# Twelve column pairs of projections move into the seven-product stage, and attention into a stage of its own

## The chip, the cores and the metric

The kernel runs on one core of one Trainium2 chip. The metric is the device time of one execution in microseconds (us). Five engines work in parallel, each through its own queue in order: TensorE (PE, matmuls, with its weight loads PEld), VectorE (DVE), ScalarE (ACT), GpSimd (POOL) and SyncE (SP, which here issues nearly all loads). All transfers share 16 DMA engines. The time before is 2117.61 us, the median of 3 runs (2116.65 to 2117.98).

## The reference, cut to what matters

One layer of a streaming encoder for 512 prompt tokens and 8 streams of 16 new tokens, together 640 columns when tokens lie along the free dimension.

```
h = rms_norm(x, g_pre)                      # 640 x 2048
p = h @ w_in                                # 13312 columns = 104 blocks of 128:
    # 6 stick-breaking heads: q, k, v, gate     24 blocks
    # 6 chunk-band heads:     q, k, v, gate     24 blocks
    # 4 memory heads:         q, gate            8 blocks
    # 3 merge gates of 2048                     48 blocks
o_sb = stick_breaking(q, k, v)   # prompt: causal; samples: 512 cached rows + 16 new
o_bd = band_softmax(q, k, v, rel_bias)      # the same lengths
o_mm = softmax_cross(q, mem_k, mem_v)       # 256 memory rows
merged = sigmoid(mg_sb) * ((o_sb * silu(g_sb)) @ w_up_sb) + ...bd + ...mm
y = x + rms_norm(merged @ w_out, g_post)
```

All is float32. Keys and values of the new tokens are outputs too, for the 12 causal heads.

## The kernel before, in words

Every float32 operand of a matmul is split into a high and a low part (`split`: ACT casts the high part, DVE subtracts), and a product is three matmuls, high by high, high by low, low by high. x lies transposed in four quarter tiles `b11`, `b12`, `b21`, `b22`: the two halves of the 2048 contraction rows by the two halves of the 640 tokens (320 each), 8 blocks of 128 rows in each.

There are two ways to project a block of 128 columns of `w_in`:

- `x_proj` (through `proj`): 16 row blocks, 3 products, 2 token halves: 96 matmuls of 128x320 into an accumulator `acc`, of which there are two. Its weights come in two loads of 512 KB into `wr`, a ring of three buffers, so one buffer feeds 48 matmuls.
- `gate_pair`: two blocks at once by Strassen's way (Winograd's form) with seven products of quarter operands, each 8 row blocks by 3 matmuls of 128x320: 168 matmuls for two blocks, where `x_proj` takes 192. It needs sums of quarter tiles of x (`t1` to `t4`) and, for every pair, sums of quarter tiles of the weights, which POOL forms (`comb`).

The stages are: a prologue (norms, memory keys and values); attention, head by head; the merge gates; the up-projections of the three branches (`up`); the output projection. In the attention stage each causal head runs `x_proj` four times (gate, v, q, k), and each memory head twice; the attention of a head is made of short matmuls that wait for ACT, DVE and POOL between them, and the projections of the next head stand between them on PE. The sums of x are formed in the heads by POOL and kept in DRAM (`t_d`). The merge gates start with four blocks by `x_proj` (`FIRST = 4`), while `t_d` is read back, and go on with 22 pairs.

The order on each engine is set by the framework's list scheduler when the kernel is built, from the dependencies, the tile buffers and some explicit `issue_after` marks; all loads of weights, caches and strips go through SP's one queue, in the order that it set. A head's caches are 16 loads of 128 KB for the keys (`kc`, two buffers of four loads each) and 8 of 256 KB for the values (`vc`).

## Time and profile before

The profiled execution took 2115.59 us, of which 2113.9 us lie between its first and last instruction (the span). The stages, by busy time of each engine in the stretch, granted PE clock (1.00 is full) and mean busy share of the DMA engines:

| stretch, us | stage | PE us (matmuls) | DVE us | ACT us | POOL us | clock | DMA share |
|---|---|---|---|---|---|---|---|
| 82 to 1101 | attention, 60 blocks by `x_proj` | 1017.32 (7779) | 473.87 | 347.36 | 140.16 | 1.00 | 0.60 |
| 1101 to 1140 | into the pairs | 32.54 (193) | 26.28 | 19.26 | 12.33 | 0.91 | 0.70 |
| 1140 to 1650 | pairs | 510.00 (3479) | 278.05 | 232.75 | 234.86 | 1.00 | 0.33 |
| 1650 to 1669 | into the up-projections | 16.02 (104) | 8.87 | 7.65 | 0.00 | 1.00 | 0.60 |
| 1669 to 1886 | up-projections | 215.87 (1463) | 117.21 | 57.72 | 57.70 | 1.00 | 0.55 |
| 1886 to 2114 | output projection | 218.82 (963) | 78.70 | 54.01 | 8.04 | 0.99 | 0.34 |

A matmul's record begins before the one ahead has ended, so its mean duration (310 ns for 128x320) is not what it costs; the number of matmuls in a stretch in which PE never waits is.

### The profile page before, as it was taken

To read this page: it belongs to the slowest core of one execution; us is meant where nothing else is said; L and a number is where in the kernel's file an instruction comes from. 1 tells how busy PE (TensorE), PEld (TensorE's weight loads), DVE (VectorE), ACT (ScalarE), POOL (GpSimd) and SP (SyncE) were. 2 spreads that over 40 slices of the span, in tenths; PEclk is the share of its full clock that TensorE was granted. 3 is DMA by queue.
4 is the path that set the end of the run, shared out by engine and by line. 5 is a ranking of instruction groups with operands and counts; after the bars stand their busy time and mean duration, and the time that the engine had idled before them with its cause. 6 is when DMAs were issued, how large, how long until landed. Compare 5 with 4: busy or idle time off the path is not lost.

```text
span 2113.9 us, 36193 instructions
## 1 busy us (share of the span) xinstructions
PE 2081.3 (98%) x14285; PEld 1975.8 (93%) x14285; DVE 1039.0 (49%) x1686; ACT 775.3 (37%) x1472; POOL 457.5 (22%) x479
## 2 busy tenths in 40 slices
PE   7999999999999999999998999999999999999998
PEld 5999999999999999999998999999999999998886
DVE  5634444544544544454356555555555434582234
ACT  6533333333333333333344444444444322232221
POOL 0001001201202200210024444444444002350000
PEclk9999999999999999999999999999999999999999
DMA  6756555745764763765545333333332655442225
GB/s 227 226 135 148 127 143 137 173 137 131 174 168 107 182 165 92 178 147 145 144 129 170 125 105 105 105 105 122 127 120 66 205 148 159 146 153 80 80 83 216
DMA packets 576153, 297.99 MB, mean 141 GB/s; under 512 B 277330, under 2 KB 537442, under 8 KB 574446
## 3 DMA queue, kind: packets, MB, share of 16 engines
q1 hardware_dynamic: 564158, 261.58, 46.0%
q0 software_dynamic: 4912, 18.37, 2.3%
q10 hardware_dynamic: 6912, 15.73, 1.9%
q8 instruction: 112, 1.84, 0.4%
q14 instruction: 59, 0.48, 0.1%
HBM read 254.18 MB, written 41.43 MB: 140 GB/s over the span
## 4 chain that ended last, share of the span: by engine, by line
PE 94%; DMA 3%; DVE 1%; ACT 1%; issue 0%; SPq 0%; DVEq 0%; ACTq 0%
PE acc L169 49%; PE q L750 25%; PE ya L156 3%; PE ya L157 3%; PE ya L155 3%; PE s L526 2%; PE o L577 1%; DMA r<-t_d 1%; PE tp L449 1%; PE acc L157 1%; DMA or<-osg_d 1%; PE acc L156 1%; PE o L156 1%; PE acc L155 1%; PE s L155 0%; PE o L155 0%
## 5 line engine op out<-in xcount | busy, mean ns | idle before, releaser
L100 DVE TENSOR_TENSOR wl<-wr,wh 128x512 fp32r<-128x512 f32 (+1 forms) x548 | 421.8, 774 | 558.0 <-ACT wh L99 554.2
L99 ACT CAST wh<-wr 128x512 fp32r<-128x512 f32 (+1 forms) x548 | 330.9, 608 | 745.9 <-PE acc L169 456.5
L169 PE MATMUL acc<-xl,wh 128*128 128x320 f32 x1920 | 452.1, 311 | 0.0
L169 PE MATMUL acc<-xh,wl 128*128 128x320 f32 x1920 | 448.5, 311 | 0.0
L169 PE MATMUL acc<-xh,wh 128*128 128x320 f32 x1920 | 441.1, 310 | 1.7 <-DVE qm L359 1.7
L169 PEld LDWEIGHTS acc<-xl,wh 128*128 128x128 f32 x1920 | 323.6, 188 | 15.3 <-issue 14.7
L169 PEld LDWEIGHTS acc<-xh,wh 128*128 128x128 f32 x1920 | 321.9, 188 | 3.9 <-DVE qm L359 2.2
L169 PEld LDWEIGHTS acc<-xh,wl 128*128 128x128 f32 x1920 | 323.1, 188 | 1.9 <-issue 1.6
L100 DVE TENSOR_TENSOR wl<-ws,wh 128x512 fp32r<-128x512 f32 x176 | 153.4, 874 | 139.7 <-ACT wh L99 139.4
L750 PE MATMUL q<-xl,wh 128*128 128x320 f32 x704 | 218.4, 310 | 1.4 <-DVE xl L100 1.4
L750 PE MATMUL q<-xh,wh 128*128 128x320 f32 x704 | 218.5, 310 | 0.3 <-ACT xh L99 0.3
L750 PE MATMUL q<-xh,wl 128*128 128x320 f32 x704 | 218.3, 310 | 0.2 <-DVE wl L100 0.2
L99 ACT CAST wh<-ws 128x512 fp32r<-128x512 f32 x176 | 109.3, 622 | 170.7 <-PE q L750 152.2
L750 PE MATMUL q<-th,wh 128*128 128x320 f32 x528 | 163.7, 310 | 4.0 <-ACT th L99 4.0
L750 PE MATMUL q<-tl,wh 128*128 128x320 f32 x528 | 163.7, 310 | 0.7 <-DVE tl L100 0.7
L750 PE MATMUL q<-th,wl 128*128 128x320 f32 x528 | 163.5, 310 | 0.0
L750 PEld LDWEIGHTS q<-xl,wh 128*128 128x128 f32 x704 | 133.2, 189 | 1.6 <-DVE xl L100 1.6
L750 PEld LDWEIGHTS q<-xh,wh 128*128 128x128 f32 x704 | 133.0, 189 | 0.6 <-ACT xh L99 0.5
L750 PEld LDWEIGHTS q<-xh,wl 128*128 128x128 f32 x704 | 133.1, 189 | 0.4 <-DVE wl L100 0.4
L155 PE MATMUL ya<-wh,gh 128*128 128x512 f32 x320 | 124.7, 390 | 0.0
L157 PE MATMUL ya<-wh,gl 128*128 128x512 f32 x320 | 124.7, 390 | 0.0
L156 PE MATMUL ya<-wl,gh 128*128 128x512 f32 x320 | 124.7, 390 | 0.0
(223 smaller groups left out, 3013.0 us busy)
## 6 DMA issues: line engine op xcount, KB each, us to landing
wr<-in_w_in_dram SPq DMA_DIRECT2D x208, 512.0 KB, 4.6
wr<-in_w_out_dram SPq DMA_DIRECT2D x32, 512.0 KB, 3.8
sig_d<-sig ACTq DMA_DIRECT2D x48, 320.0 KB, 4.4
sig<-sig_d SPq DMA_DIRECT2D x48, 320.0 KB, 3.4
kc<-in_cache_sb_k_dram SPq DMA_DIRECT2D x96, 128.0 KB, 3.3
vc<-in_cache_sb_v_dram SPq DMA_DIRECT2D x48, 256.0 KB, 4.8
kc<-in_cache_band_k_dram SPq DMA_DIRECT2D x96, 128.0 KB, 3.4
vc<-in_cache_band_v_dram SPq DMA_DIRECT2D x48, 256.0 KB, 5.5
```

The source lines that it names most:

```text
L99: ACT.copy(hi, src)
L100: DVE.tensor_tensor(lo, src, hi.bitcast(F32), op=ALU.subtract)
L155: PE.matmul(out, ah, bh, start=start, stop=False)
L156: PE.matmul(out, ah, bl, start=False, stop=False)
L157: PE.matmul(out, al, bh, start=False, stop=stop)
L169: PE.matmul(acc[:, s, :HF], a[:, k], b[s], start=first and f, stop=last and l)
L449: PE.transpose(tp[:, kb * P:(kb + 1) * P], b[:, kb * P:(kb + 1) * P], ident)
L526: return PE.matmul(s[32 * j:32 * j + 32, :nc_], qm[:, j, par * 32:par * 32 + 32], kts[j], start=par == 0, stop=par == 1, tile_position=(0, ...
L577: PE.matmul(o[32 * j:32 * j + 32, :P], l, r, start=i == 0, stop=i == len(steps) - 1, tile_position=(0, 32 * j))
L750: PE.matmul(bank_, a[:, k], b[:, k], start=first and k == 0 and n == 0, stop=k == KH - 1 and n == 2, skip_group_check=not first)
```

## The change

The chunk-band heads' 24 blocks leave `x_proj`. `gate_pair` becomes `block_pair(col, put)`, and 12 pairs for q, k, v and gate of the six chunk-band heads are run by it ahead of the 22 gate pairs; `put_raw` writes each block to DRAM (`raw_d`, 24 tensors of 320 KB), the gate block as x times its sigmoid. The whole stage of pairs moves to the front, between the prologue and attention; four gate blocks by `x_proj` stand at its start, and `sums` forms the sums of x beside them on DVE and POOL straight into the split operands, without DRAM. `t3` still takes the place of `b12`; the plain sum of b12 is kept in DRAM (`b12_d`), and the last pair takes its products in another order, reads b12 back and splits it again. The first projection of attention then starts with the second half of the rows (`back`).

In attention, a chunk-band head loads its four blocks (`loaded`) from `raw_d` in place of projecting them. `sample_att` is cut in two, `sample_score` and `sample_out`, and a head's prompt attention and scores are woven with the `sample_out` of the head before it. Heads run in the order 0, 6, 1, 7, 12, 2, 8, 3, 9, 13, 4, 5, 14, 15, 10, 11 (0 to 5 stick-breaking, 6 to 11 chunk-band, 12 to 15 memory). Buffers `b` and `e` go from 1 to 2, `l0` and the new-token tiles to 2; one of the four PSUM banks gets a tag of its own. The up-projections take the branches in the order stick-breaking, memory, chunk-band, and the first of them are free to start once the last `x_proj` matmul has been issued.

```
-B = dict(wr=3, wh=4, wl=4, kc=2, kt=4, vc=8, b=1, e=1, raw=1, q=1, k=1, v=1, wt=1)
+B = dict(wr=3, wh=4, wl=4, kc=2, kt=4, vc=8, b=2, e=2, raw=1, q=1, k=1, v=1, wt=1)
...
-    t_d = dpool.tile([4, P, KH, HF], F32, name="t_d")
+    b12_d = dpool.tile([P, KH, HF], F32, name="b12_d")
+
+    raw_d = [[dpool.tile([P, NT], F32, name=f"raw_d{n}_{h}") for h in range(6)] for n in range(4)]
...
+    def bank(name, own=False):
+
+        return ps_a.tile([P, 512], F32, tag="ps" if own else "pa", name=name, bufs=1 if own else 3)
...
+    def loaded(n, h):
+        t = pa.tile([P, NT], F32, tag=f"l{n}", name=f"l{n}", bufs=2 if n == 0 else 1)
+        SP.dma_start(t, raw_d[n][h])
+        return t
+
+    def transposed(col, n, raw):
+
+        if raw is not None:
+            return loaded(n, raw)
         acc = new_acc()
         x_proj(col, acc)
...
-    def sums(k):
-
-        r = pa.tile([P, 4, HF], F32, tag="sums", name="sums")
-        r1, r2, r3, r4 = (r[:, n] for n in range(4))
-        with tc.issue_after(last_on(POOL)):
-            for t, q in ((r1, b11), (r3, b12), (r2, b22), (r4, b21)):
-                POOL.tensor_tensor(t, q[0][:, k].bitcast(F32), q[1][:, k].bitcast(F32), op=ALU.add)
-        for t, x, y in ((r1, r3, r1), (r3, r2, r3), (r2, r2, r1), (r4, r4, r2)):
-            POOL.tensor_tensor(t, x, y, op=ALU.subtract)
-        POOL.dma_start(t_d[:, :, k].rearrange("n p c -> p n c"), r)
...
+    def sums(k):
+
+        r2, r1, r4 = (sw.tile([P, 2, HF], F32, tag="ws", name="rs", bufs=3) for _ in range(3))
+        r3 = staged(k < 6)
+        ks = slice(k, k + 2)
+        for eng, t, q in ((DVE, r1, b11), (POOL, r2, b22), (DVE, r3, b12), (POOL, r4, b21)):
+            eng.tensor_tensor(t, q[0][:, ks].bitcast(F32), q[1][:, ks].bitcast(F32), op=ALU.add)
+        POOL.dma_start(b12_d[:, ks], r3)
+        for eng, t, x, y in ((POOL, r1, r3, r1), (POOL, r3, r2, r3), (POOL, r2, r2, r1), (DVE, r4, r4, r2)):
+            eng.tensor_tensor(t, x, y, op=ALU.subtract)
+        for t, r in ((t1, r1), (t2, r2), (t4, r4)):
+            split(t[0][:, ks], t[1][:, ks], r)
+        return lambda: split(t3[0][:, ks], t3[1][:, ks], r3)
+
+    third = []
     for i in range(FIRST):
         gate(i)
+        third.append(sums(2 * i))
...
+    def put_raw(n, h):
+        def put(b, t, q):
+            if q is not None:
+                ACT.copy(t[:, :HF], q)
+            if n == 3:
+                u = sw.tile([P, NT], F32, tag="sl", name="sl")
+                ACT.activation(u, t, AF.Sigmoid)
+                POOL.tensor_tensor(u, u, t, op=ALU.mult)
+                t = u
+            POOL.dma_start(raw_d[n][h + b], t)
+        return put
+
+    pairs = [(C_BD + 768 * n + h * P, put_raw(n, h)) for n in range(4) for h in range(0, 6, 2)]
+    pairs += [(C_GATE + i * P, put_gate(i)) for i in range(FIRST, 3 * KB, 2)]
+    for n, (col, put) in enumerate(pairs):
+        block_pair(col, put, n == 0, n == len(pairs) - 1)
...
+        for h in (0, 6, 1, 7, 12, 2, 8, 3, 9, 13, 4, 5, 14, 15, 10, 11):
+            prompt, score, out = causal_head(h) if h < 12 else mem_head(h - 12)
+            interleave(rest, prompt, score)
+            rest = out
...
-        with tc.issue_after(mark if 1 < i < KB else first):
+        with tc.issue_after(mark if i > 1 else last_mm):
             proj(w_up[0], j * P, nh, o_src, acc)
```

Three places show how the order moves. The first is SP's queue around the loads of a chunk-band head (`wr` weights, `kc` cached keys, `vc` cached values, `l` a block read from `raw_d`, `natk` the prompt's keys written out). Before:

```order
L126 DMA wr<-in_w_in_dram 128x8x128 x2
L511 DMA kc<-in_cache_band_k_dram 32x32x32 x8
L126 DMA wr<-in_w_in_dram 128x8x128
L511 DMA kc<-in_cache_band_k_dram 32x32x32 x8
L126 DMA wr<-in_w_in_dram 128x8x128 x2
L504 DMA vc<-in_cache_band_v_dram 128x4x128 x8
```

And of the change, for head 9:

```order
L128 DMA wr<-in_w_in_dram 128x8x128 x2
L495 DMA kc<-in_cache_band_k_dram 32x32x32 x8
L128 DMA wr<-in_w_in_dram 128x8x128
L495 DMA kc<-in_cache_band_k_dram 32x32x32
L353 DMA l_13555<-raw_d_2_114 128x640
L495 DMA kc<-in_cache_band_k_dram 32x32x32 x6
L629 DMA out_dram<-natk 32x16x32 x4
L353 DMA l_13572<-raw_d_2_108 128x640
L495 DMA kc<-in_cache_band_k_dram 32x32x32
L546 DMA vc<-in_cache_sb_v_dram 128x4x128 x8
L128 DMA wr<-in_w_in_dram 128x8x128 x2
```

Between the two first weight loads and the last two stood one weight load, 16 key loads; now all 16 key loads, the reads of `raw_d`, the writes of `natk` and the 8 value loads of the head before stand there, with one weight load among them.

The second is PE in the prompt attention of a stick-breaking head, from the transposes `tp` of one query block over the scores `s` of the next. Before (32 projection matmuls of `acc` follow before the next `tp`, of which the first five stand here):

```order
L449 MATMUL tp<-ident,b 128x128 x2
L155 MATMUL s<-kh,qh 128x256
L156 MATMUL s<-kl,qh 128x256
L157 MATMUL s<-kh,ql 128x256
L169 MATMUL acc<-xh_79,wl 128x320
L169 MATMUL acc<-xh_75,wh 128x320
L169 MATMUL acc<-xh_79,wh 128x320
L169 MATMUL acc<-xl_76,wh 128x320
L169 MATMUL acc<-xl_80,wh 128x320
```

And of the change, in head 2, the one place of this kind in a causal head:

```order
L438 MATMUL tp<-ident,b 128x128 x2
L158 MATMUL s<-kh,qh 128x256
L159 MATMUL s<-kl,qh 128x256
L160 MATMUL s<-kh,ql 128x256
L510 MATMUL s<-kt,qm_10309 32x512 x4
L438 MATMUL tp<-ident,b 128x128
L158 MATMUL o<-wth,vh 128x256
L522 MATMUL s_13513<-knT,qr 128x128
L614 MATMUL t_13558<-ident,l_13555 128x128 x4
L510 MATMUL s<-kt,qm_10309 32x512 x4
L173 MATMUL acc<-xh_73,wh 128x320
```

No projection matmul stands between `s` and the `tp` that follows from it there, nor between that `tp` and the `o` that follows from it.

The third is POOL. Before, the sums of x stand in the heads:

```order
L659 TENSOR_TENSOR sums<-xh_73,xl_74 128x320
L659 TENSOR_TENSOR sums<-xh_77,xl_78 128x320
L659 TENSOR_TENSOR sums<-xh_79,xl_80 128x320
L659 TENSOR_TENSOR sums<-xh_75,xl_76 128x320
L661 TENSOR_TENSOR sums<-sums 128x320 x4
L662 DMA t_d<-sums 128x4x320
```

Now the last of the four sums (`rs`, `rx`) stands right ahead of the weight sums of the first pair (`ws`):

```order
L698 TENSOR_TENSOR rs<-rx,rs 128x640
L695 TENSOR_TENSOR rs<-xh_79,xl_80 128x640
L695 TENSOR_TENSOR rs<-xh_77,xl_78 128x640
L698 TENSOR_TENSOR rx<-rs,rx 128x640
L698 TENSOR_TENSOR rs<-rs 128x640
L730 TENSOR_TENSOR ws<-wr 128x512
L730 TENSOR_TENSOR ws<-wr,wr_1485 128x512
L730 TENSOR_TENSOR ws<-ws,wr 128x512 x2
```

All 20 of POOL's operations on the sums of x come ahead of the first weight sum, in the time of the four gate blocks.

More of the change, by code (lines that the diff above doesn't have):

```diff
@@ L157, in mm3, with proj @@
         PE.matmul(out, al, bh, start=False, stop=stop)
-    def proj(w, col, kn, src, acc, half=8):
-        for k0 in range(0, kn, half):
+    def proj(w, col, kn, src, acc, half=8, back=False):
+        starts = range(0, kn, half)
+        for i0, k0 in enumerate(reversed(starts) if back else starts):
             n = min(half, kn - k0)
@@ L626, in causal_head @@
-        spill(sg, i)
+        raw = h if kind == "bd" else None
+        sg = head_g(c0 + 2304 + h * P, raw)
+        vt = transposed(c0 + 1536 + h * P, 2, raw)
+        nat = pa.tile([P, 4, P], F32, tag="nat", name="nat")
+        t0 = bank("t0")
+        for t in range(4):
+            PE.transpose(t0[:, t * P:(t + 1) * P], vt[:, t * P:(t + 1) * P], ident)
+        DVE.tensor_copy(nat, t0.rearrange("p (t n) -> p t n", t=4))
+        POOL.dma_start(vp.rearrange("(t p) e -> p t e", p=P), nat)
+        vn = natural_new(vt, vs, "vn")
@@ new lines, in causal_head @@
+        qt = transposed(c0 + h * P, 0, raw)
+        kt = transposed(c0 + 768 + h * P, 1, raw)
+        v = split_v(nat)
+        qh, ql, qr = split_q(qt)
+        kh = pa.tile([P, TP], F32R, tag="kh", name="kh")
+        kl = pa.tile([P, TP], F32R, tag="kl", name="kl")
+        split(kh, kl, kt[:, :TP])
+        nat = pa.tile([P, TP], F32, tag="nat", name="natk")
+        DVE.transpose(nat, kt[:, :TP])
+        for a in range(4):
+            SP.dma_start(kp[:, 32 * a:32 * a + 32].rearrange("(c i) j -> i c j", i=32),
+                         nat[32 * a:32 * a + 32].rearrange("p (c j) -> p c j", j=32))
@@ L769, in gate_pair @@
         add(o0[:, lo], qb)
-        if i == FIRST:
+        if first:
             for f in third:
                 f()
-            fourth = [load_sum(4, t4, k, SP) for k in (0, 2)]
         product(qa, s2, t2, False)
         ACT.copy(o0[:, hi], qa)
-        if i == FIRST:
-            for f in fourth:
-                f()
-            fourth = [load_sum(4, t4, k, SP) for k in (4, 6)]
+        if last:
+            product(qa, s3, t3, False)
+            ACT.copy(o1[:, hi], qa)
+            for k in range(0, KH, 2):
+                r = staged(k % 4 == 0)
+                SP.dma_start(r, b12_d[:, k:k + 2])
+                split(b12[0][:, k:k + 2], b12[1][:, k:k + 2], r)
         qc = half()
         product(qc, s1, t1, True)
-        ACT.copy(o1[:, hi], qc)
+        if last:
+            add(o1[:, hi], qc)
+        else:
+            ACT.copy(o1[:, hi], qc)
         s4 = s2
```

252 lines of the change are left out of this document (103 added, 149 removed).

## The prediction

> **What bounds the kernel now.** I read the engines' busy time first, then the chain of work that ended last, then the stages by windows.
>
> ```profile
> PE 2081.3 (98%) x14285; PEld 1975.8 (93%) x14285; DVE 1039.0 (49%) x1686; ACT 775.3 (37%) x1472; POOL 457.5 (22%) x479
> PE 94%; DMA 3%; DVE 1%; ACT 1%; issue 0%; SPq 0%; DVEq 0%; ACTq 0%
> 82.00:1101.00 1019.00, 1017.32 (x7779) 972.02 (x7778) 473.87 (x882) 347.36 (x696) 140.16 (x260) 1.00 0.60 147
> 1200.00:1250.00 50.00, 50.00 (x343) 50.00 (x342) 26.88 (x35) 22.67 (x41) 23.89 (x17) 1.00 0.34 111
> 1100.00:1150.00 50.00, 43.54 (x268) 41.60 (x267) 35.91 (x43) 24.78 (x43) 18.91 (x13) 0.93 0.58 184
> 1650.00:1700.00 50.00, 46.91 (x313) 45.71 (x312) 20.24 (x33) 14.69 (x27) 0.00 (x0) 1.00 0.69 215
> 450.00:500.00 50.00, 49.34 (x355) 46.69 (x357) 23.90 (x43) 17.45 (x36) 3.67 (x12) 1.00 0.41 96
> 800.00:850.00 50.00, 48.97 (x398) 46.25 (x398) 23.89 (x43) 14.66 (x33) 2.55 (x9) 1.00 0.40 97
> 1750.00:1800.00 50.00, 49.36 (x333) 48.57 (x332) 20.42 (x32) 11.39 (x22) 16.65 (x10) 1.00 0.51 144
> ```
>
> PE sets the pace: 94% of the chain is PE, and in 1019 us of attention it is idle 1.7 us, nearly all of it from 450 to 500 and from 800 to 850. Where nothing else is in the stream (1200 to 1250), 343 matmuls of 128x320 pass in 50 us, so one costs **0.1458 us**. The 60 projected blocks of the attention stage are 60 x 96 x 0.1458 = 840 us of its 1019, and its attention matmuls the other 179. PE loses time at two seams: 343 - 268 = 75 matmuls or 10.9 us going into the pairs (1100 to 1150), and 343 - 313 = 30, or 4.4 us, going into the up-projections (1650 to 1700), with 1.5 us more where their second branch starts (1750 to 1800).
>
> **The change, part by part.** *Matmuls removed.* Twelve pairs take 168 where x_proj takes 192: 12 x 24 = 288 fewer, x 0.1458 = **-42.0 us**. This is on the path wherever PE stays the pace-setter. Nothing is removed from the attention matmuls.
>
> Rows for the work of POOL, for a wait that goes away, and for a DVE split that was held up beside POOL's weight sums:
>
> ```profile
> L842 POOL TENSOR_TENSOR merged<-merged,sig 128x640 f32<-128x640 f32 x32 | 59.7, 1869 | 193.4 <-DVE sig L841 177.5 <-DMA sig<-sig_d 14.4 <-issue 1.5
> L743 POOL TENSOR_TENSOR ws<-ws,wr 128x512 f32<-128x512 f32 x44 | 66.0, 1521 | 15.9 <-DVE wl L100 15.9
> 1115.64 0.63 PE L750 MATMUL q<-th,wh 128*128 128x320 f32 x1 [3.60 <-ACT th L99]
> 1094.84 5.25 DVE L100 TENSOR_TENSOR wl<-wr,wh 128x512 fp32r<-128x512 f32 x1 [1.24 <-ACT wh L99]
> ```
>
> *The longer stage of pairs.* 34 pairs x 168 x 0.1458 = 833 us. DVE, ACT and POOL are busy 27, 23 and 24 of 50 us there. A chunk-band pair does the same splits and weight sums as a gate pair; it swaps a sigmoid for a copy, and for the gate block POOL adds one product of 640 (1.9 us by the first row). POOL also issues the writes to raw_d, 2 in 24.5 us. The first two weight sums of the next pair stand ahead of these writes in POOL's queue, so I cost this at nothing; PE's 24.5 us per pair hide it. Without that cover it would be about 2 us for each of the three gate pairs.
>
> *The first seam.* Reading t_d back goes away, and with it waits like the third row; the sums of x now run beside the four gate blocks. POOL does 20 operations of 640 x 1.87 = 37 us and then four weight sums x 1.52 = 6 us before the third product of the first pair can be split. Cover: 4 x 96 x 0.1458 = 56 us of gate blocks and two products of 24, 7 us, so 63 against 43 plus the waits for the splits between the sums (each set of three buffers is used again, some 2 us x 3) and for b12_d to be written. It fits with perhaps 10 us to spare, unless DVE is held up as in the last row, where one split took 5.25 us beside POOL's work. Ends: all 10.9 us gained, or none. I take **-5 us**. At the far end of the stage b12 is read back and split under three products (10.5 us) and the 48 matmuls of the second half of the rows (7 us): nothing.
>
> *The second seam.* The order puts up-projection matmuls among the last heads, so osg is read earlier. Ends: the 4.4 and 1.5 us gained, or none: **-5 us**.
>
> *Attention with less to hide behind.* Of the 60 blocks 24 go to the pairs and the four gate blocks ahead of them, so its PE work falls to 32 x 96 x 0.1458 + 179 = 448 + 179 = 627 us. What must fit beside it:
>
> ```profile
> 1669.00:1886.00 217.00, 215.87 (x1463) 214.62 (x1464) 117.21 (x148) 57.72 (x104) 57.70 (x31) 1.00 0.55 164
> 350.00:400.00 50.00, 50.00 (x369) 48.52 (x369) 27.20 (x52) 18.36 (x39) 12.62 (x19) 1.00 0.76 182
> L100 DVE TENSOR_TENSOR wl<-wr,wh 128x512 fp32r<-128x512 f32 x516 | 408.2, 795 | 558.0 <-ACT wh L99 554.2 <-DMA out_dram<-natk 1.3
> t_d<-sums POOLq DMA_DIRECT2D x8, 640.0 KB, 5.9
> kc<-in_cache_band_k_dram SPq DMA_DIRECT2D x96, 128.0 KB, 3.4
> vc<-in_cache_band_v_dram SPq DMA_DIRECT2D x48, 256.0 KB, 5.5
> SPq L126 <- DVE wl L100: 324.2, 70, 9.6
> SPq L511 <- DVE kt L522: 82.2, 24, 8.0
> SPq L504 <- PE o L577: 34.3, 24, 6.3
> 867.89 6.24 SPq L511 DMA_DIRECT2D kc<-in_cache_band_k_dram  x8
> 875.30 7.68 SPq L511 DMA_DIRECT2D kc<-in_cache_band_k_dram  x8
> 889.33 5.98 SPq L504 DMA_DIRECT2D vc<-in_cache_band_v_dram  x8
> 898.15 0.37 SPq L126 DMA_DIRECT2D wr<-in_w_in_dram  x1
> 901.88 1.98 SPq L383 DMA_DIRECT2D out_dram<-natk  x4
> ```
>
> DVE: 474 less 112 splits (28 blocks x 4) x 0.795 = 385 us, 61% of 627. DMA: 0.60 x 1019 = 611 us of all 16 engines. The up-projections move their bytes at 0.55 / 164 = 3.35 us per MB; by that price the 28 blocks' weights (29.4 MB) take 98 us away, t_d's 5.2 MB 17 us, and reading raw_d (24 x 0.33 MB) adds 26. That leaves 522 us in 627, a share of **0.83**. The highest 50 us of attention before stood at 0.76, with PE never waiting, so 0.76 is no ceiling, but 0.83 as a mean is not shown. The work left on each queue fits; what can go wrong is its order.
>
> The order gives two bounds. From below: one causal head has no projection between its scores and its transposes, and the change from memory head 15 has a few such steps.
>
> ```profile
> 646.09 0.28 PE L157 MATMUL s<-kh,ql 128*128 128x256 f32 x1
> 648.65 0.42 DVE L464 TENSOR_TENSOR b<-b,e 128x255 f32<-128x255 f32 x1
> ```
>
> From the last score matmul to the end of the weights of a 256-wide block takes 3.0 us here; in head 2 some 11 short matmuls, 1.3 us, stand in between, and after it a 128-wide block and a split come uncovered: about 4 us there and 3 us at head 15, 7 in all. Everywhere else 4 us or more of matmuls stand in such a gap. From above: SP's stretch for a chunk-band head. I take 7 us and as much again for transfers that come late in the densest part (heads 12, 2, 8, 3, of which the three causal ones bring 4 MB of caches each): **+15 us**; ends 0 and +60 (first rival).
>
> **The sum**, against the profiled execution: -42 - 5 - 5 + 15 = -37 us on 2115.6 (span 2113.9 and 1.7 around it) is 2078.6; the median of the runs shown is 2 us above the profiled one, so **2080 us**.
>
> **The rivals.** *First, slower: weights wait behind the caches in SP's queue.* Among 16 key loads (0.87 us each by the rows), 2 reads of raw_d and one weight load (0.37), 4 writes (0.5) and 8 value loads (0.75), SP issues for 14 + 1 + 2 + 6 = 23 us with one weight load among them. Three buffers of 48 matmuls and that one give PE 28 us. If the key loads meet their longest wait (8.0 us) and the value loads theirs (6.3), it is 37 us, and with some 2 us until the data is split PE stands 11 us; six chunk-band heads make 66 us: 2117.6 - 52 + 15 + 66 = **2147 us**. It decides from 37 / 6 = 6 us per chunk-band head. For it: SP is in order, and the key buffers hold half a head (8 of 16 loads), so the later ones wait for DVE's transposes. Against: attention's own 11 us per head also feed PE, and before, SP waited 324 us for weight buffers, so it was mostly ahead.
>
> *Second, nothing stalls:* the gaps are filled, both seams close: 2117.6 - 42 - 10.9 - 5.9 = **2059 us**. For it: PE idle 1.7 us in 1019 before.
>
> *Third, the seams stay and attention loses more:* the sums of x arrive late behind POOL and DVE, up-projections still wait, and stalls are 25 us: 2117.6 - 42 + 25 = **2101 us**. For it: the 5.25 us row. Against: 20 us between 43 and 63.
>
> *Fourth, stalls that slow the clock.* After an idle time the trace shows lower clock:
>
> ```profile
> 1110.00:1125.00 15.00, 10.08 (x51) 8.59 (x50) 7.95 (x12) 6.51 (x11) 9.24 (x7) 0.89 0.59 190
> ```
>
> With the 3.60 us wait of the row above, these 15 us passed 51 matmuls of 103 at a clock of 0.89. If the 15 us of new stalls come in one or two pieces of that length, each followed by 0.11 x 15 = 1.7 us lost to the clock, and matmuls beside them stay sparse, the loss is nearer to 25 us: **2090 us**. [...]
>
> **How the numbers follow.** Chances: forecast 0.52, slower rival 0.13, nothing stalls 0.15, seams 0.12, clock 0.08. The forecast's own range, from 0 to 50 us of stalls, is 2066 to 2116; the range to the other cases takes in the second, third and fourth rivals and leaves out most of the first: 2052 to 2116. A measurement of this kernel tells 0.2%, 4 us. Faster needs less than 2113.4: all but the first rival and the forecast's and third's worst ends, 0.82; within 4 us 0.04; slower 0.14.
>
> **What would show it.** Right: 343 matmuls in each 50 us of a stage of pairs some 833 us long; attention with clock 1.00, a DMA share near 0.8 and PE waits of 10 to 20 us, the largest at heads 2 and 15; no wait of some us at the first `t2` product. The first rival shows as PE waiting for ACT or DVE splits of `wr` in attention, ahead of it SP waiting for `kc` or `vc` buffers; the third as waits for `tl`, `th` or `ws` at the start of the pairs, and for `oh` at the up-projections. The forecast is wrong if attention takes over 665 us, or if the pairs pass fewer than 343 matmuls per 50 us.

## The result, and the profile after

The changed kernel takes **2135.3 us** (median; 2131.4 to 2138.2) against 2117.3 us of the kernel before on the same chip: a ratio of 1.0084, 95% interval [1.0066, 1.0101]. It is 0.8% slower; 2080 us was forecast, and the range ended at 2116. The profiled execution took 2134.1 us, its span is 2132.4.

The page of the changed kernel, engines and chain of waits:

```profile
PE 2058.5 (97%) x13997; PEld 1945.9 (91%) x13997; DVE 1128.3 (53%) x1788; ACT 815.5 (38%) x1567; POOL 599.0 (28%) x557
PE 85%; issue 4%; DMA 4%; DVE 2%; POOL 2%; SPq 2%; ACT 1%; DVEq 0%; POOLq 0%; ACTq 0%
```

The 288 matmuls are gone (14285 - 13997), but PE's share of the chain fell from 94% to 85%: PE waits now. Where it does is read from the windows of the changed kernel (stretch; PE, PEld, DVE, ACT, POOL busy; granted clock, DMA share, GB/s), by stage first:

```profile
78.00:134.40 56.40, 56.40 (x386) 56.36 (x386) 47.03 (x38) 22.44 (x35) 40.42 (x26) 1.00 0.45 144
134.40:980.80 846.40, 842.23 (x5714) 841.25 (x5714) 477.96 (x590) 375.40 (x670) 424.24 (x307) 0.99 0.35 112
980.80:1614.10 633.30, 604.33 (x4686) 560.00 (x4685) 315.84 (x624) 219.58 (x472) 56.95 (x150) 0.98 0.71 165
1614.10:1764.00 149.90, 126.50 (x988) 115.69 (x987) 85.50 (x179) 49.33 (x111) 9.32 (x26) 0.92 0.76 199
1764.00:1905.10 141.10, 140.66 (x959) 140.40 (x958) 70.60 (x102) 39.47 (x70) 55.71 (x32) 1.00 0.58 167
...
500.00:550.00 50.00, 50.00 (x343) 50.00 (x343) 26.48 (x34) 23.07 (x41) 23.87 (x17) 1.00 0.34 111
100.00:150.00 50.00, 45.83 (x286) 45.06 (x285) 46.40 (x34) 19.53 (x33) 40.37 (x22) 0.90 0.35 111
1100.00:1150.00 50.00, 41.43 (x275) 38.96 (x274) 21.52 (x47) 14.19 (x31) 3.18 (x8) 0.90 0.91 204
1650.00:1700.00 50.00, 37.24 (x264) 34.72 (x265) 26.47 (x53) 11.48 (x29) 2.64 (x7) 0.85 0.90 224
```

The rows are: four gate blocks, pairs, attention up to the last projected block, its last heads with up-projections among them, the rest of the up-projections. Inside the pairs 343 matmuls pass per 50 us, as forecast. From 100 to 150, where the pairs begin, 57 are missing (8.3 us). Attention and up-projections take 924 us (980.8 to 1905.1). Worked out for them were 627 us and the 217 us of the row from 1669 to 1886 before, but that row holds 1463 of the 1536 matmuls of the up-projections; with the other 73, at 0.1458 us each, it is 627 + 228 = 855, so **some 69 us are lost**. PE stands idle for 53 of them (29.0 + 23.4 + 0.4, from the busy times). That leaves about 16 for the lower clock, 0.98 over 633 us and 0.92 over 150. So the whole gain of the pairs, and some, goes into attention.

What PE waits for from 1100 to 1150 must be read through two queues. PE's waits name a softmax, but the chain of waits of the changed kernel goes on behind it (start, duration, piece):

```profile
1112.19 0.11 PE o L158
1112.29 5.73 DMA vc<-in_cache_band_v_dram
...
1118.09 5.28 DMA wr<-in_w_in_dram
...
1126.46 0.36 DVE b L463
```

and the timelines of DVE and of ACT there show both idle for 14.3 us ahead of the same weight split (in brackets the idle time and what ended it):

```profile
1124.11 0.69 DVE L102 TENSOR_TENSOR wl<-wr,wh 128x512 fp32r<-128x512 f32 x1 [14.35 <-ACT wh L101]
1124.72 0.42 DVE L432 SCALAR_TENSOR_TENSOR b<-s,strip 128x256 f32<-128x256 f32 x1
```

```profile
1123.46 0.62 ACT L101 CAST wh<-wr 128x512 fp32r<-128x512 f32 x1 [14.29 <-DMA wr<-in_w_in_dram]
```

The scores were ready (PE had passed them by 1112.7); their softmax stood behind the split of a weight slab in DVE's in-order queue, and that slab's load had only been issued at 1118.09. SP's timeline of the changed kernel says why:

```profile
1059.73 17.15 SPq L128 DMA_DIRECT2D wr<-in_w_in_dram  x3
1080.90 6.93 SPq L495 DMA_DIRECT2D kc<-in_cache_sb_k_dram  x8
1087.92 3.17 SPq L598 DMA_DIRECT2D st<-rext_d  x6
1091.19 8.53 SPq L495 DMA_DIRECT2D kc<-in_cache_sb_k_dram  x4
1099.82 1.10 SPq L594 DMA_DIRECT2D st<-rext_d  x1
1101.03 0.97 SPq L495 DMA_DIRECT2D kc<-in_cache_sb_k_dram  x2
1102.09 2.40 SPq L629 DMA_DIRECT2D out_dram<-natk  x4
1104.53 1.38 SPq L495 DMA_DIRECT2D kc<-in_cache_sb_k_dram  x2
1105.95 1.56 SPq L594 DMA_DIRECT2D st<-rext_d  x3
1107.61 5.48 SPq L546 DMA_DIRECT2D vc<-in_cache_band_v_dram  x8
1113.15 2.76 SPq L594 DMA_DIRECT2D st<-rext_d  x4
...
1118.09 1.01 SPq L128 DMA_DIRECT2D wr<-in_w_in_dram  x2
```

SP has issued the weight loads of the first row by 1076.9, and the next one follows at 1118.1. In these 41 us stand 4 us of waiting for a key buffer, key loads (17.8 us of issuing, 5.75 of them in one load), value loads (5.5), writes (2.4) and 16 small strip loads (9.5). The three weight buffers feed 3 x 48 matmuls, 21 us, and attention's own work 11 us at most; then everything behind the weights stands.

Not all of the idle time is of this kind. Three such stretches in attention are longer than 28 us: 41 us (here), 36 us from 1300 and 57 us from 1591. Inside them and in the 10 us after each, PE stands idle for 9.5, 0.9 and 19.6 us, 30 of the 52 us that it is idle from 981 to 1764. The middle one costs next to nothing. Elsewhere the chain of waits runs through late cache loads themselves, as here, where PE then stood idle for 4.3 us:

```profile
1208.39 6.99 DMA kc<-in_cache_sb_k_dram
```

A key load takes 3.4 us in the median of the run; this one, and another of 6.77 us at 1420.65, landed late, their transposes on DVE came late (DVE idles 2.96 us ahead of those at 1215.39), and what stood behind those in DVE's queue came late for PE.

### The profile page after: what moved, and what is told of

The parts are those of the page before. It is cut to its first block, busy times and chain, and to the rows that moved or that the text cites. A ratio compares the mean times of both kernels' runs of the same rounds, so it can differ in the third digit from the quotient of the medians.

```text
span 2132.4 us, 36113 instructions
## 1 busy us (share of the span) xinstructions
PE 2058.5 (97%) x13997; PEld 1945.9 (91%) x13997; DVE 1128.3 (53%) x1788; ACT 815.5 (38%) x1567; POOL 599.0 (28%) x557
## 3 DMA queue, kind: packets, MB, share of 16 engines
q1 hardware_dynamic: 541310, 265.51, 46.4%
## 4 chain that ended last, share of the span: by engine, by line
PE 85%; issue 4%; DMA 4%; DVE 2%; POOL 2%; SPq 2%; ACT 1%; DVEq 0%; POOLq 0%; ACTq 0%
PE q L737 39%; PE acc L173 26%; PE ya L160 3%; PE ya L158 3%; PE ya L159 3%; PE s L510 1%; POOL merged L864 1%; PE o L569 1%; SPq L495 1%; DMA kc<-in_cache_sb_k_dram 1%; PE tp L438 1%; PE acc L158 1%; PE acc L160 1%; DVE wl L102 1%; PE acc L159 1%
## 5 line engine op out<-in xcount | busy, mean ns | idle before, releaser
L737 PE MATMUL q<-xh,wl 128*128 128x320 f32 x1088 | 338.1, 311 | 4.2 <-DVE wl L102 4.2
L737 PE MATMUL q<-xl,wh 128*128 128x320 f32 x1088 | 337.6, 310 | 0.0
L173 PE MATMUL acc<-xh,wl 128*128 128x320 f32 x1152 | 271.5, 313 | 0.0
L173 PE MATMUL acc<-xh,wh 128*128 128x320 f32 x1152 | 269.2, 313 | 0.0
L173 PE MATMUL acc<-xl,wh 128*128 128x320 f32 x1152 | 269.1, 312 | 0.0
L173 PEld LDWEIGHTS acc<-xh,wh 128*128 128x128 f32 x1152 | 194.4, 189 | 10.4 <-issue 7.5
L173 PEld LDWEIGHTS acc<-xl,wh 128*128 128x128 f32 x1152 | 194.9, 190 | 6.3 <-issue 6.3
L173 PEld LDWEIGHTS acc<-xh,wl 128*128 128x128 f32 x1152 | 195.2, 190 | 2.8 <-issue 2.3
L730 POOL TENSOR_TENSOR ws<-wr 128x512 f32<-128x512 f32 x102 | 148.6, 1470 | 80.0 <-DVE wl L102 78.0
L737 PEld LDWEIGHTS q<-th,wl 128*128 128x128 f32 x816 | 153.2, 188 | 0.2 <-DVE wl L102 0.2
```

Of the source, the lines that this page charges most:

```text
L173: PE.matmul(acc[:, s, :HF], a[:, k], b[s], start=first and f, stop=last and l)
L730: eng.tensor_tensor(o, a[c], b[c], op=op)
L737: PE.matmul(bank_, a[:, k], b[:, k], start=first and k == 0 and n == 0, stop=k == KH - 1 and n == 2, skip_group_check=not first)
```

## The experiments

Two theories of the loss, which the texts on record put at 80 us: **S**, supply (weights, strips and caches come too late for so little PE work), and **C**, chains (the two interleaved heads' own dependencies). All edits are to the changed kernel, and all ratios to the kernel before, timed beside each. The order on every queue is set anew by the list scheduler for each kernel, so an edit that changes costs or buffers also moves instructions.

**1. Half of the move.** Values and gates stay in the pairs; queries and keys go back to `x_proj`:

```
-        qt = transposed(c0 + h * P, 0, raw)
-        kt = transposed(c0 + 768 + h * P, 1, raw)
+        qt = transposed(c0 + h * P, 0, None)
+        kt = transposed(c0 + 768 + h * P, 1, None)
-    pairs = [... for n in range(4) for h in range(0, 6, 2)]
+    pairs = [... for n in (2, 3) for h in range(0, 6, 2)]
```

> Undoes half of the move: only the value and gate projections of the chunk-band heads stay in the stage of pairs, their query and key projections go back to x_proj in attention (the same result). It gives back 6 x 24 x 0.1458 = 21 us of matmuls and returns 12 x 14 = 168 us of projections to attention. Theory S (attention is starved: the transfers, in the order in which SP issues them, do not come in time for so little PE work): DMA 522 + 42 of weights - 13 of raw reads = 551 us in 795, a share of 0.69 instead of 0.83, so most of the 80 us lost between the start of attention and the output projection go: 2135 + 21 - 65 = 2091 us, 2080 to 2105. Theory C (the chains within two interleaved heads starve PE, whatever the transfers do): the loss stays with the heads, 2135 + 21 = 2156 us; above 2140 speaks for C.

Measured: 2096.0 us, 0.9903 [0.9888, 0.9917]; S said 2091, C 2156. Half of the move is faster than the kernel before and than all of it. A window of this kernel from within attention, in which PE is idle for 4 of 600 us:

```profile
900.00:1500.00 600.00, 595.64 (x4643) 559.17 (x4642) 294.71 (x566) 223.74 (x449) 52.49 (x143) 1.00 0.66 155
```

This does not yet decide between the theories: two blocks more in a head give its loads more time, and they also fill the gaps of its chains.

**2. One cache load per head.**

```
-        for b_ in range(NB):
-            t = pa.tile([P, 4, P], F32, tag="vc", ...)
-            SP.dma_start(t, cv[b_]...)
-            vcs.append(t)
+        t = pa.tile([P, 4, P], F32, tag="vc", ...)
+        SP.dma_start(t, cv[0]...)
+        vcs = [t] * NB
 # and kc = load_k(0) once ahead of the loop, instead of four times in it
```

> Leaves out most cache transfers: each head loads one of its four key pieces and one of its eight value caches and uses it for all (other values are computed, the instructions of PE, DVE and ACT stay the same). Theory S: with about 52 MB less to move, attention loses less than 15 us instead of 80: 2060 to 2075 us. Theory C: the loss stays, above 2115 us.

Measured: 2078.9 us, 0.9821 [0.9805, 0.9837]. Without the cache transfers 56 us come back, with as many instructions as before on PE, DVE and ACT (13997, 1788 and 1567): S carries most of the loss. It is 4 us above S's range, though. Bytes, issues and waits for cache buffers go together here, so the run does not tell which of them it is.

**3. The sums of x on DVE alone.**

```
-        for eng, t, q in ((DVE, r1, b11), (POOL, r2, b22), (DVE, r3, b12), (POOL, r4, b21)):
+        for eng, t, q in ((DVE, r1, b11), (DVE, r2, b22), (DVE, r3, b12), (DVE, r4, b21)):
 # and the four subtractions on DVE as well
```

> Moves all sums of x beside the four gate blocks from POOL to DVE (the same result). Theory P (the first seam is late because DVE runs its splits at 1.4 to 2.1 us instead of 0.8 beside POOL's sums): DVE's 32 sums cost 26 us in a window of 56 that then holds 16 x 0.8 of weight splits and 16 x 0.82 of sum splits, 52 in all, and the 58 matmuls or 8.5 us lost between 125 and 150 mostly come back: 2127 to 2131 us. Rival (there is simply too much for DVE before the third product): the same or slower, 2134 to 2142 us.

Measured: 2125.3 us, 1.0050 [1.0033, 1.0067], 10 us less. DVE's groups from 100 to 150 us (busy, mean ns of one), of the changed kernel:

```profile
L102 DVE TENSOR_TENSOR wl<-wr,wh 128x512 fp32r<-128x512 f32 x11 | 20.2, 1849 | 1.5 <-ACT wh L101 1.4
```

and of this kernel, with its window:

```profile
L102 DVE TENSOR_TENSOR wl<-wr,wh 128x512 fp32r<-128x512 f32 x11 | 8.6, 786 | 0.4 <-ACT wh L101 0.4
```

```profile
100.00:150.00 50.00, 50.00 (x343) 50.00 (x342) 47.59 (x54) 22.68 (x37) 18.42 (x12) 1.00 0.40 122
```

Beside POOL's sums (POOL busy 40.4 of 50 us) one weight split takes 1849 ns; without them, with POOL still busy 18.4 us, 786. DVE does 20 operations more in the stretch in nearly the same busy time, 47.6 us where it was 46.4, and the seam closes. What it is in POOL's sums that holds the splits up, these runs do not show.

**4. Keys issued from POOL's queue** (`POOL.dma_start` for `SP.dma_start` in `load_k`).

> Issues the key cache loads from POOL's queue instead of SP's (the same result and bytes). Theory Q (weights stand behind key loads in SP's in-order queue, which wait for buffers or are slow to issue, 1.7 us each in places): weights are issued in time and at least half of the 80 us goes: 2090 to 2105 us. Theory B (the 16 DMA engines themselves are full in these stretches, at shares of 0.8 to 1.04): the order of issue changes little, 2125 to 2145 us; if POOL is slow to issue, more.

Measured: 2133.1 us, 1.0070 [1.0050, 1.0089]: no gain clear of the noise, as B had it, but not for B's reason alone. POOL's busy time rises from 599 to 790 us, and PE's waits for softmaxes from 16 to 21 us. Inconclusive for SP's queue.

**5. Half of the move and the sums on DVE.** The edits of 1 and 3.

> Both at once: value and gate projections of the chunk-band heads in the pairs, query and key projections in attention, and all sums of x on DVE (the same result). If the two losses are separate (the seam at 125 to 150 us, and starved attention), the gains add: 2096 - 7 to 10 = 2087 us, 2083 to 2091. If an earlier start of the pairs is given back later, 2094 us or more.

Measured: 2089.1 us, 0.9874 [0.9859, 0.9888]: 7 us below the half alone. The two losses are separate, as the first forecast had it.

**6. Keys in longer runs.** Each of the four loads of a key tile reads 512-byte rows of a half of one stream instead of 128-byte pieces of two.

> Reads as many bytes of key caches in as many loads, but in runs of 512 bytes instead of 128 (so the keys arrive in another order and the scores of the sample rows are others). By packet times of 13.0 and 28.7 ns, the 16 engines' time for keys falls from 213 to about 118 us. Theory B (the DMA engines are too full in bursts): 95 of the about 262 us of engine time that the run with one cache per head took away, which gave 56 us, so 20 us: 2115 us, 2108 to 2122. Theory W (the key loads wait for buffers that DVE's transposes free, the transfer's own time does not matter): 2129 to 2138.

Measured: 2145.2 us, 1.0135 [1.0117, 1.0154]; neither theory. SP's transfers of the changed kernel and of this one (packets, MB, share of 16 engines):

```profile
q1 hardware_dynamic: 541310, 265.51, 46.4%
```

```profile
q1 hardware_dynamic: 369278, 265.51, 43.3%
```

The engines are relieved by 0.464 x 2132 - 0.433 x 2142 = 62 us, and the time rises by 10. So their time over the whole run is not what attention lacks, and theory B falls as it was stated. But SP's issuing of the keys became shorter as well (for the 96 loads of the stick-breaking heads 58.7 us in all instead of 98.5, by SP's timelines), while a key load lands later (in the median 4.5 us instead of 3.6 for these heads, 4.1 instead of 3.7 for the chunk-band heads), and the order moved. So SP's issuing time alone does not set the loss either, and why this kernel is slower stays open.

**7. A third key buffer** (`kc=3`, and one buffer for the query tile).

> Three key buffers instead of two; for room, one query buffer instead of two (the same result). Theory W (SP stands at key loads until DVE's transposes free a buffer, and weights behind it come late): 2112 to 2125 us. Theory B (full DMA engines): the same, 2130 to 2138.

Measured: 2179.6 us, 1.0298 [1.0282, 1.0313], 44 us *slower* than the change, and neither theory. SP's order where the keys of the first chunk-band head begin, in the changed kernel:

```profile
1027.12 13.28 SPq L128 DMA_DIRECT2D wr<-in_w_in_dram  x3
1040.66 2.98 SPq L495 DMA_DIRECT2D kc<-in_cache_band_k_dram  x3
```

and in this one:

```profile
1025.14 5.80 SPq L495 DMA_DIRECT2D kc<-in_cache_band_k_dram  x4
1031.06 0.49 SPq L128 DMA_DIRECT2D wr<-in_w_in_dram  x1
```

Keys are issued earlier, ahead of weights. Near the end SP issues no weight load for 129 us:

```profile
1592.77 0.62 SPq L128 DMA_DIRECT2D wr<-in_w_up_sb_dram  x1
1593.96 4.66 SPq L546 DMA_DIRECT2D vc<-in_cache_mem_v_dram  x8
...
1722.34 0.43 SPq L128 DMA_DIRECT2D wr<-in_w_up_sb_dram  x1
```

In that stretch SP also waits for results of the last heads (the longest waits are 13.7, 12.5 and 11.8 us), so a part of it belongs to the heads' chains. And the query tile lost a buffer in the same run; which of the two changes of buffers costs the 44 us was not tried.

**8. Another order of heads**: `(0, 6, 1, 7, 2, 8, 3, 9, 4, 10, 5, 11, 12, 13, 14, 15)`.

> Another order of heads only: stick-breaking and chunk-band heads in turn, the four memory heads last (the same result); so the chunk-band heads 10 and 11 no longer stand together at the end, where PE loses some 35 of the 80 us between 1600 and 1700. Theory S: without projections two heads with 8 MB of caches cannot be fed, spread they can: 2108 to 2122 us. Theory C, or a loss that only moves to another pair of heads: 2128 to 2140.

Measured: 2166.2 us, 1.0241 [1.0215, 1.0266], slower than both theories. With heads of both kinds in turn, SP goes six times for 38 to 45 us without a weight load, once for each chunk-band head. The chunk-band heads starve one by one; a neighbour with four projections does not save them.

Runs 6, 7 and 8 pointed at one quantity, read from SP's timeline of each kernel: the stretches between two weight loads (`wr`) in attention, all its rows from the first head to the last, and what they exceed 28 us by, summed. The 28 us are the first rival's three buffers and one, 21 + 7, a threshold that no run measures. The table has all kernels, in the order of that sum; runs 9 to 18 follow below, and "all three" stands for the edits of strips, sums and values. The last column is what a run takes beyond its own matmuls with nothing stalled (2059 us for the full move, 2069 for three quarters, 2080 for half: 2117.6 - 16.8 - 1.75 per moved block), less 10 where the sums are on POOL.

| kernel | longest, us | summed beyond 28 us | us | lost |
|---|---|---|---|---|
| before | 20.4 | 0 | 2117 | - |
| 14, half, all three | 30.5 | 3 | 2083 | 3 |
| 12, half, strips, sums | 31.0 | 3 | 2085 | 5 |
| 18, one cache per head, strips, sums | 32.1 | 4 | 2072 | 13 |
| 2, one cache per head | 32.2 | 4 | 2079 | 10 |
| 5, half, sums | 32.8 | 5 | 2089 | 9 |
| 1, half | 33.4 | 5 | 2096 | 6 |
| 13, strips, sums and values | 37.3 | 9 | 2107 | 48 |
| 9, one strip load | 48.2 | 20 | 2107 | 38 |
| 17, strips, sums | 48.3 | 20 | 2097 | 39 |
| 4, keys from POOL's queue | 42.7 | 21 | 2133 | 64 |
| 16, strips from POOL's queue | 49.8 | 22 | 2122 | 53 |
| 10, three quarters, sums | 51.3 | 23 | 2112 | 43 |
| 11, three quarters, strips, sums | 56.2 | 28 | 2092 | 23 |
| 15, three quarters, all three | 57.2 | 29 | 2093 | 24 |
| 6, keys in longer runs | 51.0 | 35 | 2145 | 76 |
| the change | 57.4 | 50 | 2135 | 66 |
| 3, sums | 56.9 | 52 | 2125 | 66 |
| 8, other order of heads | 44.8 | 73 | 2166 | 97 |
| 7, third key buffer | 128.9 | 128 | 2180 | 111 |

The sum separates the kernels that lose little (13 us at most, at sums up to 5) from the two that lose most, but between them it orders nothing: at sums from 20 to 35 the loss goes from 23 to 76. So long stretches without a weight load go with large losses, and they are not all of the loss. Nor is it a proof, since these kernels differ in more than this.

**9. One strip load instead of 16** per chunk-band head; POOL copies the second strip out of the first.

```
-            for bb in range(NB):
-                SP.dma_start(st1[bb * TS:(bb + 1) * TS], ext_ap(h, 128, [[1, TS], [1, 512]]))
...
-            for bb in range(NB):
-                SP.dma_start(st3[bb * TS:(bb + 1) * TS], ext_ap(h, 112, [[1, TS], [0, NB], [1, TS]]))
+            SP.dma_start(stw, ext_ap(h, 112, [[0, NB], [1, TS], [1, TS + 512]]))
+            st1 = stw[:, TS:]
```

> The change as it is, but each chunk-band head reads its sample strips with one load of 128x528 instead of 16 small ones, and POOL copies the second strip out of the first (the same result). Theory Q (a chunk-band head without projections is as long as SP's stretch for it, and 15 issues of 0.35 to 0.5 us fewer shorten that by 5 to 7 us in each of six heads): 2095 to 2108 us. Theory B (the cache bytes set the stretch, not the number of issues): 2128 to 2138.

Measured: 2106.6 us, 0.9951 [0.9934, 0.9968]: **28.7 us** with 90 small issues fewer, in theory Q's range. The stretch shown above, in this kernel's timeline of SP:

```profile
1077.39 0.37 SPq L128 DMA_DIRECT2D wr<-in_w_in_dram  x1
1081.77 5.83 SPq L495 DMA_DIRECT2D kc<-in_cache_sb_k_dram  x8
1088.53 0.39 SPq L128 DMA_DIRECT2D wr<-in_w_in_dram  x1
...
1103.94 0.43 SPq L128 DMA_DIRECT2D wr<-in_w_in_dram  x1
1104.47 7.90 SPq L546 DMA_DIRECT2D vc<-in_cache_band_v_dram  x8
1112.45 0.78 SPq L128 DMA_DIRECT2D wr<-in_w_in_dram  x1
```

Weights come every 8 to 15 us again. Fewer issues are not all that changed: the scheduler also set two weight loads, at 1088.53 and 1103.94, among the key loads and ahead of the value loads, where the change has none before 1118.09. So the 28.7 us are those of the issues and of the new order together. The strips' bytes cannot be the cause: over the run they are 1.9 MB. Nor were the DMA engines too full in this stretch, as the windows of the change and of this kernel show:

```profile
1075.00:1125.00 50.00, 42.43 (x345) 37.48 (x343) 22.07 (x41) 12.68 (x28) 5.37 (x13) 0.97 0.69 156
```

```profile
1075.00:1125.00 50.00, 50.00 (x400) 44.36 (x399) 30.54 (x61) 18.21 (x41) 6.05 (x16) 1.00 0.86 190
```

With the weights in time PE never stands, at a DMA share of 0.86 instead of 0.69.

**10 to 12. Three quarters, and the strips with less than the full move.** Query projections back in attention, sums on DVE; the same with one strip load; and the half with sums and one strip load.

> Three quarters of the move, with the sums on DVE: key, value and gate projections of the chunk-band heads in the pairs, their query projection in attention (the same result). Theory L (a chunk-band head loses what its caches take beyond its PE work; one block adds 14 us to 11): against 2089 with two blocks left, -10.5 us of matmuls and 6 to 18 us of stalls, 2085 to 2097 us. If the loss grows evenly with what is moved: halfway between 2089 and 2125, 2107.

> Three quarters of the move, the sums on DVE and the strips in one load each. Theory Q: SP's stretch shrinks below what one block and attention cover, 2075 to 2085 us. Theory B: as without the strips' change, within 3 us.

> Half of the move, the sums on DVE and the strips in one load each. With two blocks left per chunk-band head all theories see little to gain: 2083 to 2090 us, against 2089 without the strips' change.

Measured: 2112.3 us (0.9973 [0.9962, 0.9984]), 2091.9 (0.9881 [0.9868, 0.9894]) and **2084.8** (0.9844 [0.9832, 0.9857]). The strips give 20 us at three quarters and 4 at half: the more projections remain in a head, the less SP's stretch matters. At three quarters theory Q's 2075 to 2085 was missed, and theory B's "within 3 us" too; the last stretch stays at 56 us. For the first, theory L's 2085 to 2097 was missed as well; a loss that grows evenly, 2107, was nearer.

**13 to 15. Values of four streams in one load**, with sums and strips, at full, half and three quarters of the move.

```
-            SP.dma_start(t, cv[b_].rearrange("(k p) e -> p k e", p=P))          # 8 of 256 KB
+            SP.dma_start(t, cv[b_:b_ + 4].rearrange("b (k p) e -> p (b k) e", p=P))   # 2 of 1 MB
```

> The whole move with three things that take work out of the way at the same bytes: sums on DVE, the strips in one load each, and the value caches of four streams in one load (2 loads of 1 MB per head instead of 8 of 256 KB, in as many buffer bytes). The result is the same. Theory Q (SP's in-order issue): from 2107 us, -7 at the first seam and -3 to -5 us for each head whose six saved issues (0.79 us each) lay on the path, 2070 to 2085. Theory B (the transfers' own time): only the seam, 2096 to 2102; slower where a larger load lands later.

> The same with half of the move (query and key projections in attention). 2085 us without the value loads' change, 2080 if nothing stalls: 2080 to 2086 by both theories.

> The same with three quarters of the move (the query projection in attention). 2092 us without the value loads' change, 2070 if nothing stalls. Theory Q: 2072 to 2084. Theory B: 2088 to 2095.

Measured: 2107.3 us (0.9964 [0.9951, 0.9976]), **2083.1** (0.9844 [0.9830, 0.9857]) and 2093.5 (0.9895 [0.9882, 0.9909]). Six issues fewer per head gave nothing at half and three quarters, and cost 10 us at full (against run 17). That is outside both forecasts at full, where the half came out as forecast and three quarters as theory B had it. The number of issues alone is not the law. Transfers, changed kernel and run 13 (median us from issue to landing last):

```profile
vc<-in_cache_sb_v_dram SPq DMA_DIRECT2D x48, 256.0 KB, 5.8
```

```profile
vc<-in_cache_sb_v_dram SPq DMA_DIRECT2D x12, 1024.0 KB, 8.8
```

A load four times as large lands 3 us later, and PE's waits for softmaxes in run 13 grow to 22.6 us in 11 pieces; that the one causes the other was not tried.

**16. Strips issued from POOL's queue**, 16 per head as before.

> The change as it is, with the 16 small strip loads of each chunk-band head issued from POOL's queue instead of SP's (the same result, the same transfers). Theory Q: SP's stretch is as short as with one load, 2100 to 2115 us. Theory B (many small transfers are slow, whoever issues them): 2128 to 2140.

Measured: 2122.0 us, 1.0025 [1.0014, 1.0035]: 13 of the 28.7 us. It lies between the theories. The bytes are the same, so taking the strips out of SP's queue is worth 13 us, with what POOL's queue costs taken off; here too the scheduler then put two weight loads among the keys and ahead of the values. POOL's transfers take more of the engines (changed kernel, then this one):

```profile
q0 software_dynamic: 6000, 22.30, 2.8%
```

```profile
q0 software_dynamic: 9072, 24.28, 5.0%
```

**17 and 18. What is left at the full move.** Sums and strips with the caches as they are, and with one cache per head as in run 2.

> The whole move with the sums on DVE and the strips in one load each; the value caches are read in eight loads per head again (the same result). If the first seam's gain is additive: 2107 - 7 to 10, 2097 to 2100 us, and loading four streams at once had cost 7 to 10 us. If what the pairs gain is given back in attention: 2104 to 2110.

> Leaves out most cache transfers as before (each head loads one key piece and one value cache and uses them for all), with the sums on DVE and the strips in one load each. If all that is lost comes from transfers and their issue: 2059 to 2066 us, as the second rival has it. If the heads' own chains lose something as well: 2068 to 2078.

Measured: 2097.4 us (0.9907 [0.9892, 0.9922]) and 2072.0 (0.9785 [0.9768, 0.9801]), the first as an additive seam has it, the second in the range in which the heads' own chains lose something as well. The seam's gain is additive (9.2 after the strips, 10.0 alone). So of the 76 us between the measured 2135 and the 2059 without stalls, taken away in this order, about 29 go with the strips, 9 with the seam and 25 with the caches, and 13 remain. The order matters: taken away first, in run 2, the caches are worth 56, and strips and sums after them 7 together. So caches and strips are not two separate losses; with either of them gone the other costs less, which fits loads that stand in one queue ahead of the weights. What remains with neither, 13 us, is all that is left for C in that kernel; single waits of PE there after 500 us are no longer than 3.0 us.

The half with all three edits, 2083.1 us, is the fastest of the kernels that leave nothing out: 1.6% below the kernel before and 2.4% below the change. It and run 12 do not differ measurably.

## Why the prediction was wrong, by its own steps

- **Matmuls removed, -42.0 us: right.** 288 fewer, and 343 per 50 us throughout the pairs.
- **The longer stage of pairs at nothing extra: nearly right.** 846 us against 833, 8 of the 13 at its start. The other 5 are the price of a matmul: a window of 50 us also counts those on its edges, and the 5665 matmuls from 150 to 980.8 took 0.1467 us each where 0.1458 was reckoned.
- **First seam, -5 us: wrong.** Its loss is 8.3 us from 100 to 150 where it was 10.9. The sum set POOL's 43 us against a cover of 63 and named DVE's hold-up, the 5.25 us row, as a reservation only. With POOL's sums beside them DVE's splits cost 1849 ns instead of 795, and DVE was busy 47 of the 56 us. Moving *more* work to DVE was the cure: 10 us.
- **Second seam, -5 us: cannot be told apart.** The up-projections begin among the last heads, which lose the most (23.4 us of idle PE from 1614 to 1764). From 1764 on nothing is lost.
- **New stalls, +15 us, ends 0 and +60: the step that failed.** The term was sized by gaps in two heads' own chains, 7 us, and as much again; SP's queue was left to a rival at a chance of 0.13. Measured are some 66 us (76 above the time without stalls, less 10 at the first seam), above the upper end. The mechanism is in the main the first rival's, weights behind caches in SP's queue; late cache loads themselves come on top. Its time, 2147 us, was nearer than the forecast, but it counted six chunk-band heads at 11 us, where the trace has two long stretches that cost 9.5 and 19.6 us of idle time, some 23 us of it elsewhere, and about 16 us of lower clock.
- **The first rival's price, 23 us for SP's stretch against 28 us of cover, was short of its largest omission.** Its list had 16 key loads, 2 reads of raw_d, 4 writes and 8 value loads, but not the 17 strip loads that a chunk-band head issues too. The trace of before had them:

```profile
st<-rext_d SPq DMA_DIRECT2D x48, 32.0 KB, 3.7
st<-rext_d SPq DMA_DIRECT2D x48, 8.0 KB, 5.3
...
898.61 1.96 SPq L607 DMA_DIRECT2D st<-rext_d  x4
```

 96 loads, 16 per head, at 1.96 / 4 = 0.49 us: 7.8 us. 23 + 7.8 = 31 us is above the 28 of cover by itself, and with the rival's 2 us until the data is split PE stands 5 us in each of six heads: 2117.6 - 52 + 15 + 30 = 2111 us instead of 2080, before any longer wait. The stretch shown above is 41 us.
- **"Attention's own 11 us per head also feed PE" was no help.** Attention's splits and softmaxes stand behind the weight splits in the queues of ACT and DVE (14.3 us idle in both), so a late weight stops them too.
- **"SP waited 324 us for weight buffers, so it was mostly ahead" was a mean, and of the old kernel.** Projections stood in every head there, and the longest stretch without a weight load was 20.4 us. From 980 to 1765 of the changed kernel SP waits 93 us for weight buffers in all, and still leaves PE without weights in the stretches above.
- **The mean DMA share: too high, and without use.** 0.83 was forecast; 0.71 and 0.76 were measured in the two stretches of attention. Where PE lost most, from 1100 to 1150 and from 1650 to 1700, the share was 0.91 and 0.90, but a high share alone does not stop PE: in run 9 it never stands from 1075 to 1125 at 0.86.
- **Fourth rival, stalls that slow the clock: lower clocks stand beside and behind idle times, and were underpriced.** The clock was 0.90 and 0.85 in the two windows of 50 us in which PE idled 8.6 and 12.8 us, and 0.95 in the one right behind the second, where it never idled; from 150 to 1050, with no idling, it was 1.00 in every one. But it was 0.97 from 1600 to 1650, at 10.6 us of idling, and 1.00 from 1150 to 1200, at 3.5: how much clock an idle time costs was not shown. Of the 69 us lost about 16 are left for it beside 53 of idling; 10 were allowed.
- **What would show the forecast wrong** was named as attention over 665 us, and for the first rival waits for splits of `wr`. Both are seen: 627 + 69 us, and one wait of 11.6 us for ACT's part of the split of a weight, PE's longest in attention, at the end of the last long stretch. Elsewhere the second comes under another name, as a wait for a softmax.

What stays open: how the loss divides between SP's issuing time, the order that the scheduler set and late landings, since runs 2, 9, 16 and 18 change more than one of them and runs 4 and 6 took issuing time off SP without a gain; and what the last 13 us are.

## What to carry to other kernels

A saving on the busiest engine is worth its size only while the work that stays behind still covers the in-order queue that feeds it (here half of the move, 21 us of matmuls, brought 21 us, and all of it, 42 us, cost 18): list every issue of that queue for the section that loses its cover, the small ones too, and compare the longest stretch without the critical load with what the buffers hold. When cover is the limit, try a part of the move: here half of it with the sums on DVE and fewer loads is 2083 us, all of it with the same edits 2107, all of it alone 2135. A wait that names a quick operation may be a wait for what stands ahead of it in its queue: here a softmax whose scores stood ready by 1112.7, behind a weight split for which DVE idled 14.35 us.

## What the runs showed of the hardware that was not expected

- A DVE split of 128x512 takes 786 ns without POOL's sums of x and 1849 ns beside them (additions of 128x640), so giving POOL half of the sums made the whole later.
- A third key buffer, with one query buffer fewer, made the kernel 44 us slower: keys are issued ahead of weights, and 129 us pass without a weight load.
- Reading the keys in runs of 512 bytes relieved the DMA engines by 62 us and the time rose by 10.
- Issued from POOL's queue, strip loads of 2 MB are 3072 packets and raise that queue's share of the engines from 2.8% to 5.0%, some 46 us of their time (0.050 x 2120 - 0.028 x 2132). From SP's queue the same bytes were 8448 packets, and that queue's share fell from 46.4% to 46.2% without them, some 10 us by these rounded shares.
